# Attention on one core: VectorE's share of the output products put off behind the exchange of maxima, value operands split one place later

## The chip, the core and the metric

The kernel runs on one core of one Trainium2 chip. The core has five engines that work in parallel, each through its own instructions in program order: TensorE (PE; its weight loads are listed as PEld), VectorE (DVE), ScalarE (ACT), GpSimd (POOL) and SyncE (SP), which here does nothing but issue DMA transfers. They wait for one another by semaphores. TensorE reads operands from the on-chip SBUF and writes sums to banks of PSUM. The metric is the time of one execution on the device in microseconds (us); smaller is better.

## The reference

One decoder block over 2048 positions and 1024 channels. The normalized input is multiplied by one wide matrix; from its columns come a recurrent branch and an attention branch, which are projected, merged with sigmoid gates, projected again, added to the input and normalized. What matters here is the attention: eight heads of 128 channels; each position attends to three key sets, windows of 128, 512 and 2048 positions with strides of 1, 4 and 16, and the three results are merged by their softmax denominators:

```
for window, dilation in ((128, 1), (512, 4), (2048, 16)):
    s = q @ kk * HEAD_DIM ** -0.5, masked to the band
    lse = logsumexp(s);  o = exp(s - lse) @ vv
w = softmax(stack(lses));  out = sum(w * stack(outs))
y_attn = (out * silu(z_attn)) @ w_out_attn
merged = sigmoid(g_r + bg_r) * y_rnn + sigmoid(g_a + bg_a) * y_attn
```

Everything is in float32. The kernel holds each operand of a matmul as a pair: a rounded high part and the rest as a low part. One product is then three matmuls (high by high, high by low, low by high).

## The kernel before, in words

A *split* makes such a pair: one engine writes the rounded copy (line 162 on ScalarE, 165 on VectorE), another subtracts it from the original (line 168 on POOL, 171 on VectorE). Because these are helpers, most splits of the kernel carry the same four lines, and the name of the tile tells them apart. `mm3` (lines 156 to 159) issues the three matmuls.

The change lies in the attention stage, about 1375 to 1935 us of the execution. Its order is written out by hand: instructions go to each engine in the order in which the Python program issues them. The main loop (lines 2286 to 2311) runs over steps `s`. There are 16 half heads (`Head` objects: eight heads, each for two halves of the sequence), and each has six units, in the order of `ORDER`: four of kind "c" (one residue of the position modulo 4, which serves the windows of 512 and 2048) and two of kind "w" (the window of 128). In step `s`, TensorE does the scores of unit `s`; VectorE takes their maxima (line 1595) and ScalarE the exponentials (line 1596); seven steps later the probabilities are scaled (line 1660) and transposed (lines 1680 and 1693), and one step after that multiplied with the values (`sums`) into a bank `o`, which VectorE empties by a multiplication with a gate (lines 1719 and 1739).

Work that belongs to a place of a step is listed in a plan by `at(step, place, function)` and issued by `run`. The places in a step, in order:

- HEAD: before the scores of the step;
- SOFTMAX: after the step's maxima and exponentials;
- then most of the step's share of output products (below);
- EXCHANGE: once per half head, that is in every sixth step; one matmul sends the maxima and sums of each key set to the partitions where the other set needs them (`exchange`, line 1752), VectorE reads them (line 1761) and forms the common maxima (`maxima`), ScalarE takes their exponentials (line 1775);
- then the rest of the step's output products;
- WEIGHTS: in the same sixth step, VectorE turns them into the factors `M` (`weights`, lines 1777 to 1784);
- transposes of unit `s - 7` and sums of unit `s - 8`;
- TAIL: among other things the scaling of the unit that is transposed in the next step, and loads.

Keys and queries are split at HEAD and SOFTMAX places (`split_kq`, tiles kraw and kq); at HEAD of two steps POOL regroups the queries of the window of 128 (`window_queries`, line 1557). Values of a unit are loaded (`load_v`, line 1563, one transfer; `load_v1`, line 1581, four) into one of three raw tiles, vraw, in TAIL of the step that is three before their transposes, and split (`split_v` into vh, `split_v1` into wh; ScalarE rounds, POOL subtracts) at TAIL of the step before their transposes. All these loads are issued by SP, one after the other, so a load whose tile is still in use holds up those behind it.

TensorE's spare time in the stage is filled with the *output products* (generator `steps`, from line 1833): y_rnn and y_attn as 128 by 512 tiles, each of eight steps of one `mm3` into a PSUM bank `pj`. `spend` issues as many as are owed: 3.6 per step of the attention, later 3.1. In the course of a tile, at fixed steps, the generator also issues

- the emptying of the tile before: VectorE multiplies its bank with the loaded gate (line 1913) and, for y_attn, adds the other branch's part (line 1915);
- the store of that tile (line 1920) and the load of the next gate (line 1908), both by SP;
- weight loads (line 367), and row loads and splits of the next group's rows (`load_y`, line 1887 or 373; `split_y`, lines 1889 to 1897): ScalarE rounds into yh, and VectorE or POOL, by the row's number, subtracts into yl.

After the attention stage the same generator goes on inside `output_products`.

Of the kernel before, what the change touches and what calls it, by code (L numbers as in the profile page):

```python
# [15 lines left out]
ALU = mybir.AluOpType  # L16
# [73 lines left out]
def decoder_block(ctx, tc, x, c, positions, g_norm, w_mod, b_mod, w_in, b_gate, conv_w, conv_b,  # L90
# [76 lines left out]
    def lo_pool(o, i, h):  # L167
        nc.gpsimd.tensor_tensor(o, i, h.bitcast(F32), ALU.subtract)  # L168

    def lo_dve(o, i, h):  # L170
        nc.vector.tensor_tensor(o, i, h.bitcast(F32), ALU.subtract)  # L171
# [1353 lines left out]
    def at(slot, place, fn, *args):  # L1525
        plan.setdefault((slot, place), []).append((fn, args))

    def run(slot, place):
        for fn, args in plan.pop((slot, place), ()):
            fn(*args)  # L1530

    class Head:
# [273 lines left out]
        def enlist(self, B):  # L1806
            for c, (ld, s, place) in enumerate(((5, 2, HEAD), (5, 2, SOFTMAX), (4, 1, HEAD), (3, 0, HEAD))):
                at(B - ld, TAIL, self.load_kq, c)
                at(B - s, place, self.split_kq, c)
            for i, s in enumerate((B, B + 2)):  # L1810
                at(s, HEAD, self.window_queries, i)
            e = B + NU
            at(e - 1, SOFTMAX, self.gather, 1)
            at(e, HEAD, self.gather, 0)
            at(e, EXCHANGE, self.exchange)
            at(e, EXCHANGE, self.maxima)
            at(e, EXCHANGE, self.exponentials)
            at(e, WEIGHTS, self.weights)
            for u, (kind, x) in enumerate(ORDER):
                s = B + u + LAG  # L1820
                at(s - 1, TAIL, self.scale, kind, x)
                at(s - 1, TAIL, self.split_v if kind == "c" else self.split_v1, x)
                at(s - 3, TAIL, self.load_v if kind == "c" else self.load_v1, x)
            e = B + NU + LAG
            at(B + LAG - 1, TAIL, self.load_gate)
            at(e, TAIL, self.merge, 1)
            at(e + 1, TAIL, self.merge, 3)
            at(e + 2, TAIL, self.store)
# [4 lines left out]
    def steps(jobs):  # L1833
# [55 lines left out]
        def split_y(j, k):  # L1889
            if j < len(jobs):  # L1890
                w, ys, n = jobs[j]
                t = Y0.pop((ys is yaT, n, k), None)
                yh, yl = Y.get((j, k)) or new_y(j, k)
                t = yl[:].bitcast(F32) if t is None else t[:]
                hi_act(yh[:], t)
                on_dve = k not in (3, 4) if j == LAST_HEAD else k % 2 or not j
                (lo_dve if on_dve else lo_pool)(yl[:], t, yh[:])

        def load_g(t):
            j, m = tiles[t]  # L1900
# [9 lines left out]

        def evict(t, ps):
            g = G[t]
            nc.vector.tensor_tensor(g[0][:], ps[:], g[0][:], ALU.mult)
            if len(g) > 1:
                nc.vector.tensor_tensor(g[0][:], g[0][:], g[1][:], ALU.add)

        def store(t):
            j, m = tiles[t]
            w, ys, n = jobs[j]
            nc.sync.dma_start((mrT if ys is yaT else meT)[m * P : (m + 1) * P, n * CH : (n + 1) * CH], G.pop(t)[0][:])  # L1920
# [5 lines left out]
        for t, (j, m) in enumerate(tiles):  # L1926
            ps = T(pj, [P, CH], F32, "pj") if j < LAST_HEAD or t % 4 < 2 else FP["bank"](t % 4 - 2)
            for k in range(KT):
                u = 2 * t + k // KH
                if k % KH == 1:  # L1930
                    if u + 3 < RAW_W - 1:
                        if u + 3 == n_w[0]:
                            load_w(u + 3)
                    elif u == 2 * KT * LAST_HEAD:
                        load_w(RAW_W - 1)
                    if u in raw_at:
                        load_w(raw_at[u])
                    if u in split_at:
                        split_w(split_at[u])
                if k == (1 if j < LAST_HEAD else 3) and t:  # L1940
                    evict(t - 1, last)
                if k == (4 if t == TURN else 3) and t < TURN + 3:
                    load_g(t)
                if k == (7 if j < LAST_HEAD else 6) and t:
                    store(t - 1)
                x = 2 * (KT * min(j, LAST_HEAD) + m) + k // KH
                wt = W[x]
                row = {5: 7, 6: 5, 7: 6}.get(k, k) if t == TURN + 1 else k
                yh, yl = Y[j, row]
                mm3(ps[:], wt[:, 0, row % KH, :], wt[:, 1, row % KH, :], yh[:], yl[:], first=k == 0, last=k == KT - 1)  # L1950
                if k % KH == KH - 1 and (j != LAST_HEAD if m < KT - 1 else j <= LAST_HEAD):
                    W.pop(x)

                step = m * KT + k
                if j < LAST_HEAD:
                    if step in range(KT * KT - 24, KT * KT - 14, 2):
                        load_y(j + 1, (step - KT * KT + 24) // 2)
                    if step == KT * KT - KT - 1:
                        split_y(j + 1, 0)
                    if m == KT - 1:  # L1960
                        if k < 4:
                            split_y(j + 1, k + 1)
                        if j + 1 < LAST_HEAD:
                            if 4 <= k < KT - 1:
                                load_y(j + 1, k + 1)
                        else:
                            if k == 1:
                                load_y(j + 1, 5)
                            if k == 3:
                                load_y(j + 1, 6)  # L1970
                                load_w(n_w[0])
                                load_y(j + 1, KT - 1)
                            if k == KT - 1:
                                split_y(j + 1, KT - 1)
                    if j and m == 0 and k in (0, 2, 3):
                        split_y(j, 5 + (k + 1) // 2)
                else:
                    i = (t - KT * LAST_HEAD) * KT + k
                    if i < 2:
                        split_y(j, 5 + i)  # L1980
                    if i in (0, 1, 2, 3, 5, 6, 7, 8):
                        load_y(LAST_HEAD + 1, i - (i > 3))
                    if i in (4, 5, 6, 7, 10, 11, 12, 13):
                        split_y(LAST_HEAD + 1, i - (4 if i < 8 else 6))
                    if k == KT - 1 and TURN + 2 <= t < len(tiles) - 1:
                        load_g(t + 1)
                yield
            last = ps
# [2 lines left out]

    LAST_HEAD, RAW_W = NB + 2, 2 * KT * (NB + 2) + 4
    n_steps = [0]

    def spend(fill, owed, left):

        while owed >= left + 1:
            next(fill)
            n_steps[0] += 1
            owed -= 1  # L2000
        return owed
# [274 lines left out]
    with tc.manual_schedule():  # L2276
        units = []
        for g in range(2 * H):
            hd = Head(g // H, g % H)
            hd.enlist(NU * g)  # L2280
            units += [(hd, u) for u in ORDER]
        last_head = [hd]
        owed = 0.0
        first = min(s for s, _ in plan)
        end = max(s for s, _ in plan) + 1
        for s in range(first, max(end, len(units) + LAG + 1)):
            rate = FILL[0] if s < NU * H + LAG else FILL[1]
            owed += rate + (MORE if 0 <= s <= NU else 0.0)

            run(s, HEAD)  # L2290
            softmax = None
            if 0 <= s < len(units):
                hd, u = units[s]
                softmax = hd.scores(*u)
            if softmax:
                softmax()
            run(s, SOFTMAX)
            owed = spend(fill, owed, rate / 4)
            run(s, EXCHANGE)
            owed = spend(fill, owed, 0.0)  # L2300
            run(s, WEIGHTS)
            if 0 <= s - LAG < len(units):
                hd, u = units[s - LAG]
                hd.transposes(*u)
            owed = spend(fill, owed, 0.0)
            if 0 <= s - LAG - 1 < len(units):
                hd, u = units[s - LAG - 1]
                evict = hd.sums(*u)
                if evict:
                    at(s + 1, SOFTMAX, evict)  # L2310
            run(s, TAIL)
        owed = spend(fill, (NB + 2) * KT * KT - n_steps[0], 0)
        pools.close("ap", "sc", "pT", "po")
        output_products(fill)
# [29 lines left out]
```

## Time and profile before

| | us |
|---|---|
| three runs | 2197.92, 2202.35, 2202.59 |
| their median | 2202.35 |
| the profiled execution | 2203.34 |
| its span, first to last instruction | 2200.7 |
| TensorE busy | 2161.4 (98%) |
| VectorE, ScalarE, POOL busy | 1488.3, 1261.9, 1237.5 |

The profile is one execution. A page gives the busy time of each engine over the span and the groups of instructions by line; further views answer for a stretch of time: who waited for whom, the instructions of an engine in order of time with the idle time before each and what ended it, and busy time with TensorE's granted clock (1.00 is full speed) by window. A busy TensorE is not TensorE at its peak, because overlapping matmuls are counted to their ends.

### The profile page before, as it was taken

The page shows a single profiled execution, that of the slowest core. Times are in us where ns is not written, and L with a number is a line of the kernel's source. Part 1 is how long each engine was busy: PE and PEld are TensorE (multiplying, and loading weights), DVE is VectorE, ACT ScalarE, POOL GpSimd, SP SyncE. Part 2 cuts the span into 40 slices and gives each one's busy share as a digit, 9 for nine tenths or more (in the row PEclk, how much of TensorE's full clock was granted, in tenths as well). Part 3 has the DMA queues.
Part 4 walks back from the last instruction along what each step waited for, and adds up shares of the span by engine and source line. Part 5 has one row for each costly group of instructions (what it writes and reads, how often), then busy time and mean ns, then how long its engine had stood idle before and what let it go on. Part 6 is the DMA issues. An engine that isn't in the chain of part 4 may idle for free. (4 is left out here: it accounts for less than half of the span.)

```text
span 2200.7 us, 34270 instructions
## 1 busy us (share of the span) xinstructions
PE 2161.4 (98%) x11330; PEld 1838.1 (84%) x11330; DVE 1488.3 (68%) x2453; ACT 1261.9 (57%) x2543; POOL 1237.5 (56%) x910
## 2 busy tenths in 40 slices
PE   8999999999999999999999999999999999999998
PEld 5998888888888998888888887888889898978786
DVE  6678888978576765455545465467677878755876
ACT  4647667667543447557557412567778887632433
POOL 2468767677566355445445223446575656433886
PEclk9999999999999999999999999999999999999999
DMA  8355665665897567787887898989988888799453
GB/s 291 103 172 185 219 198 194 203 209 195 265 274 221 166 191 255 248 250 233 263 258 248 263 286 274 284 267 273 289 272 270 242 257 255 226 291 296 160 164 134
DMA packets 454522, 513.89 MB, mean 234 GB/s; under 512 B 91241, under 2 KB 333637, under 8 KB 453577
## 3 DMA queue, kind: packets, MB, share of 16 engines
q1 hardware_dynamic: 427444, 431.81, 65.2%
q10 hardware_dynamic: 26708, 79.86, 9.4%
q8 instruction: 89, 1.46, 0.3%
q14 instruction: 89, 0.72, 0.1%
q0 software_dynamic: 192, 0.05, 0.0%
HBM read 337.52 MB, written 174.07 MB: 232 GB/s over the span
## 5 line engine op out<-in xcount | busy, mean ns | idle before, releaser
L168 POOL TENSOR_TENSOR S<-R,S 128x512 fp32r<-128x512 f32 x278 | 411.4, 1485 | 372.2 <-ACT S L162 271.2
L154 PE MATMUL V<-T,S 128*128 128x512 f32 x1344 | 324.4, 390 | 0.5 <-DVE xr L482 0.5
L154 PE MATMUL X<-T,S 128*128 128x512 f32 x1344 | 323.3, 389 | 0.3 <-POOL S L168 0.3
L154 PEld LDWEIGHTS X<-T,S 128*128 128x128 f32 x1344 | 252.0, 188 | 52.9 <-POOL S L168 0.7
L154 PEld LDWEIGHTS V<-T,S 128*128 128x128 f32 x1344 | 251.4, 188 | 52.9 <-DVE xr L482 1.0
L154 PE MATMUL pj<-yh,S 128*128 128x512 f32 x848 | 287.6, 397 | 4.4 <-ACT yh L162 3.8
L168 POOL TENSOR_TENSOR S<-s,S 128x512 fp32r<-128x512 f32 x114 | 183.0, 1605 | 103.2 <-ACT S L162 78.7
L162 ACT ACTIVATE S<-R 128x512 fp32r<-128x512 f32 x278 | 171.2, 622 | 117.1 <-DMA R<-in_w_in_dram 77.4
L154 PEld LDWEIGHTS pj<-yh,S 128*128 128x128 f32 x848 | 160.7, 190 | 37.5 <-ACT yh L162 4.7
L1596 ACT ACTIVATE pp<-pp,st 128x256 f32<-128x256 f32 (+3 forms) x256 | 133.4, 523 | 75.4 <-DVE st L1595 75.0
L154 PE MATMUL pj<-yl,S 128*128 128x512 f32 x424 | 167.5, 395 | 2.4 <-DVE yl L171 1.5
L154 PE MATMUL Y<-T,S 128*128 128x512 f32 x672 | 161.5, 389 | 0.0
L154 PE MATMUL W<-T,S 128*128 128x512 f32 x672 | 161.5, 389 | 0.0
L154 PE MATMUL Z<-T,S 128*128 128x512 f32 x672 | 161.4, 389 | 0.0
L154 PEld LDWEIGHTS Z<-T,S 128*128 128x128 f32 x672 | 126.1, 188 | 26.2
L154 PEld LDWEIGHTS Y<-T,S 128*128 128x128 f32 x672 | 126.1, 188 | 26.2
L154 PEld LDWEIGHTS W<-T,S 128*128 128x128 f32 x672 | 126.1, 188 | 26.2
L162 ACT ACTIVATE S<-s 128x512 fp32r<-128x512 f32 x114 | 71.1, 624 | 117.2 <-DVE s L299 61.6
L998 DVE SCALAR_TENSOR_TENSOR xc<-xr,par,xc 128x512 f32<-128x512 f32 x96 | 97.9, 1020 | 50.6 <-ACT xc L992 48.3
L171 DVE TENSOR_TENSOR ptl<-pT,pth 128x384 fp32r<-128x384 f32 (+1 forms) x160 | 97.8, 627 | 49.3 <-ACT pth L162 47.1
L1595 DVE CUSTOM_DVE_ANT_0 pp<-sc,msk 128x256 f32<-128x256 f32 (+3 forms) x256 | 104.2, 449 | 34.7 <-PE sc L154 32.1
L168 POOL TENSOR_TENSOR kq<-kraw,kq 128x512 fp32r<-128x512 f32 (+1 forms) x64 | 101.3, 1594 | 39.8 <-ACT kq L162 30.2
(393 smaller groups left out, 4828.7 us busy)
## 6 DMA issues: line engine op xcount, KB each, us to landing
sD<-S ACTq DMA_DIRECT2D x112, 512.0 KB, 3.6
S<-sD SPq DMA_DIRECT2D x112, 512.0 KB, 4.8
S<-wD SPq DMA_DIRECT2D x100, 512.0 KB, 5.9
R<-in_w_in_dram SPq DMA_DIRECT2D x195, 256.0 KB, 4.2
wD<-s ACTq DMA_DIRECT2D x64, 256.0 KB, 4.5
T<-in_w_mod_dram SPq DMA_DIRECT2D x8, 1024.0 KB, 9.5
vN<-ev SPq DMA_DIRECT2D x64, 128.0 KB, 2.6
zaT<-ev SPq DMA_DIRECT2D x32, 256.0 KB, 3.4
```

Source lines behind the costliest of these rows:

```text
L154: nc.tensor.matmul(o, lhsT=l, rhs=r, start=st, stop=sp, **kw)
L162: nc.scalar.activation(o, i, AF.Copy)
L168: nc.gpsimd.tensor_tensor(o, i, h.bitcast(F32), ALU.subtract)
L171: nc.vector.tensor_tensor(o, i, h.bitcast(F32), ALU.subtract)
L998: nc.vector.scalar_tensor_tensor(xc, xr[:, i : i + CH], cw(i), xc, ALU.mult, ALU.add)
L1595: nc.vector.tensor_tensor_reduce(pdst, s_ps, mask, 1.0, 3e38, ALU.add, ALU.min, m_)
L1596: nc.scalar.activation(pdst, pdst, AF.Exp, bias=m_, scale=-1.0, accum_out=l_)
```

## The change

It has two parts.

First, between the place SOFTMAX and the end of WEIGHTS of a step that has an exchange, VectorE's instructions of the output products are not issued where the generator reaches them, but kept in a list: the low part of a split row (line 171 as called from `split_y`) and the emptying of a finished tile (lines 1913 and 1915). They are issued right after WEIGHTS, in their order, or earlier if a product is about to read such a row or a store is about to send such a tile. Rounding on ScalarE, subtractions on POOL, loads and stores stay where they were. In all other steps nothing is put off.

Second, the values of a unit are split at the place SOFTMAX of the step of their transposes, and not at TAIL of the step before. Their loads stay where they were.

```
             for u, (kind, x) in enumerate(ORDER):
                 s = B + u + LAG
                 at(s - 1, TAIL, self.scale, kind, x)
-                at(s - 1, TAIL, self.split_v if kind == "c" else self.split_v1, x)
+                at(s, SOFTMAX, self.split_v if kind == "c" else self.split_v1, x)
                 at(s - 3, TAIL, self.load_v if kind == "c" else self.load_v1, x)
...
                 on_dve = k not in (3, 4) if j == LAST_HEAD else k % 2 or not j
-                (lo_dve if on_dve else lo_pool)(yl[:], t, yh[:])
+                if on_dve:
+                    on_vector((j, k), lambda: lo_dve(yl[:], t, yh[:]))
+                else:
+                    lo_pool(yl[:], t, yh[:])
...
         def evict(t, ps):
             g = G[t]
-            nc.vector.tensor_tensor(g[0][:], ps[:], g[0][:], ALU.mult)
-            if len(g) > 1:
-                nc.vector.tensor_tensor(g[0][:], g[0][:], g[1][:], ALU.add)
+
+            def gated():
+                nc.vector.tensor_tensor(g[0][:], ps[:], g[0][:], ALU.mult)
+                if len(g) > 1:
+                    nc.vector.tensor_tensor(g[0][:], g[0][:], g[1][:], ALU.add)
+            on_vector(t, gated)

         def store(t):
+            settle(t)
...
                 row = {5: 7, 6: 5, 7: 6}.get(k, k) if t == TURN + 1 else k
+                settle((j, row))
                 yh, yl = Y[j, row]
...
+    put_off, waiting = [False], []
+
+    def on_vector(key, fn):
+        if put_off[0]:
+            waiting.append((key, fn))
+        else:
+            fn()
+
+    def settle(key=None):
+        while waiting and (key is None or any(key == k for k, _ in waiting)):
+            waiting.pop(0)[1]()
...
             run(s, SOFTMAX)
+            put_off[0] = (s, EXCHANGE) in plan
             owed = spend(fill, owed, rate / 4)
             run(s, EXCHANGE)
             owed = spend(fill, owed, 0.0)
             run(s, WEIGHTS)
+            put_off[0] = False
+            settle()
```

## The prediction

> **What bounds the kernel now.** I read four views, in this order: the page, the list of waits of TensorE inside the attention stage, a table of short windows, and the timelines of the engines around each place where TensorE stood. The page first:
>
> ```profile
> span 2200.7 us, 34270 instructions
> PE 2161.4 (98%) x11330; PEld 1838.1 (84%) x11330; DVE 1488.3 (68%) x2453; ACT 1261.9 (57%) x2543; POOL 1237.5 (56%) x910
> ```
>
> TensorE sets the time, so the change can only win what TensorE loses in the stage that it touches, the attention stage from 1375 to 1935 us. Its waits there (engine, line, what released it: us in total, times, longest):
>
> ```profile
> PE pT L1680 <- ACT pp L1660: 2.3, 2, 2.0
> PE sc L154 <- POOL q L1557: 1.5, 3, 0.7
> PE sc L154 <- DVE sm L1748: 1.4, 1, 1.4
> PE sc L154 <- DVE xq L1761: 1.4, 1, 1.4
> PE pj L154 <- POOL yl L168: 0.9, 1, 0.9
> PE pT L1680 <- DVE ptl L171: 0.7, 1, 0.7
> PE o L154 <- DVE zt L1719: 0.4, 1, 0.4
> ```
>
> That is all there is to win directly: 8.6 us in ten stops. The windows show what two of them cost besides (window, its length, then busy us of PE, PEld, DVE, ACT and POOL, granted clock, DMA share, GB/s):
>
> ```profile
> 1438.00:1442.00 4.00, 4.00 (x14) 3.38 (x15) 3.35 (x19) 2.69 (x10) 0.90 (x2) 0.57 0.96 344
> 1834.00:1838.00 4.00, 4.00 (x21) 3.96 (x20) 1.83 (x6) 4.00 (x13) 2.20 (x2) 0.57 0.25 74
> ```
>
> After the stops at 1437 and 1832 the granted clock of the next 4 us is 0.57: each costs another 0.43 x 4 = 1.72 us.
>
> On this the Trainium skill, page "TensorE: Matmul & The Clock Gate", section "The HAM clock gate (the "warmup" mystery)", says that the clock is halved after at least one idle window of about 3.4 us. The trace differs: stops of 1.4 and 2.3 us were enough. By the page's rule these two terms of 1.72 would be absent and the sum below 3.44 us smaller.
>
> **The two stops behind an exchange.** Rows of TensorE, VectorE and ScalarE in order of time (start, length, engine, line, instruction, in brackets the idle time before it and what ended it). First the exchange step at 1434, then the one at 1824:
>
> ```profile
> 1433.93 0.68 DVE L1739 TENSOR_TENSOR yw<-o,zt 128x512 f32<-128x512 f32 x1
> 1435.82 1.70 DVE L171 TENSOR_TENSOR yl<-yl,yh 128x512 fp32r<-128x512 f32 x1 [1.21 <-ACT yh L162]
> 1437.44 0.34 DVE L1761 TENSOR_TENSOR xq<-sc,cs 128x64 f32<-128x64 f32 x2
> 1437.93 1.25 PE L154 MATMUL sc<-kq,q 128*128 128x256 f32 x6 [1.41 <-DVE xq L1761]
> 1439.70 0.17 DVE L1784 SCALAR_TENSOR_TENSOR M<-M,dm 128x16 f32<-128x16 f32 x1
> ```
>
> ```profile
> 1824.11 0.38 PE L154 MATMUL sc<-sm,msk 128*128 128x128 f32 x2
> 1825.67 1.19 DVE L171 TENSOR_TENSOR yl<-R,yh 128x512 fp32r<-128x512 f32 x1 [1.45 <-ACT yh L162]
> 1826.78 0.34 DVE L1761 TENSOR_TENSOR xq<-sc,cs 128x64 f32<-128x64 f32 x2
> 1828.84 0.68 DVE L1913 TENSOR_TENSOR fg<-pj,fg 128x512 f32<-128x512 f32 x1
> 1829.55 0.69 DVE L1915 TENSOR_TENSOR fg<-fg,fg 128x512 f32<-128x512 f32 x1
> 1832.04 0.18 DVE L1784 SCALAR_TENSOR_TENSOR M<-M,dm 128x16 f32<-128x16 f32 x1
> 1832.25 1.23 ACT L1660 ACTIVATE pp<-pp,M 128x384 f32<-128x384 f32 x2 [1.68 <-DVE M L1784]
> 1832.96 0.30 PE L1680 MATMUL pT<-cs,pp 128*128 128x128 f32 x1 [2.04 <-ACT pp L1660]
> ```
>
> Both show one thing: VectorE works in program order, and an output product's subtraction (line 171, tile yl) stands in front of the maxima. VectorE idles until ScalarE has rounded that row, then subtracts, and only then reads the exchanged maxima (line 1761), though they had been in PSUM since 1824.5 in the second case. There a product's eviction (lines 1913 and 1915) also stands in front of the weights (line 1784).
>
> **Part 1: putting off.** Nothing is added or removed: instructions of lines 171, 1913 and 1915 that fall between the softmax and the weights of an exchange step go behind the weights. I ran the loop's own arithmetic (3.6, later 3.1 product steps per attention step): 7 of the 16 exchange steps have such work (steps 12, 18, 30, 36, 42, 66 and 84); in the other 9 nothing changes. The stops above belong to steps 12 and 84.
>
> Step 12: from the first exchanged maximum to the last weight takes 1437.44 to 1439.87, so 2.43 us undisturbed. Without the subtraction in front it can start when VectorE's earlier work (line 1739) ends at 1434.6, 2.8 us sooner. The scores bank is then free before TensorE wants it, near 1436.5. Gain: 1.41 + 1.72 = 3.13 us. What it costs: the subtraction, 1.2 to 1.7 us, now ends near 1438.5, and the product that reads that row comes just there; I put this at nothing, with 0.5 as its worst end.
>
> Step 84: maxima from about 1824.6, weights by 1827.1, the scaling (1.23 us) done by 1829; TensorE wants the transposes at 1830.9. There is 1.9 us of cover, so even a chain stretched by POOL stays hidden. Gain: 2.04 + 0.27 (a second stop of the same kind, the 2.3 of the list) + 1.72 = 4.03 us. Behind the weights now stand 1.2 + 0.68 + 0.69 us of put-off work, then the rest of the step: no later than before, since the whole chain moved up by 5 us. The store of that product waits for its eviction, but comes six product steps after it, over a step of attention.
>
> In the other five steps the chain gets shorter where nothing waited for it: nothing.
>
> **Part 2: the values split later.** Per unit (96 of them) two instructions move: ScalarE's rounding and POOL's subtraction. They carry no DMA. They move past, on ScalarE, the rounding of keys and the step's exponentials; on POOL, the subtractions of keys and the regrouping of window queries (line 1557). What that frees, by POOL's rows before the stop at 1721 (TensorE 0.70, and 0.33 at 1619):
>
> ```profile
> 1717.59 1.30 POOL L168 TENSOR_TENSOR vh<-vraw,vh 128x512 fp32r<-128x512 f32 x1 [1.78 <-ACT vh L162]
> 1718.85 1.84 POOL L168 TENSOR_TENSOR kq<-kraw,kq 128x768 fp32r<-128x768 f32 x1
> 1720.63 1.63 POOL L1557 CAST q<-kq 128x512 fp32r<-128x512 f32 x2
> 1721.76 2.02 PE L154 MATMUL sc<-kq,q 128*128 128x256 f32 x12 [0.70 <-POOL q L1557]
> ```
>
> With the 1.30 us of values behind instead of ahead, the queries end about 1 us sooner, for ScalarE's rounding of the keys comes 0.5 us sooner too. Gain: 0.55 of the 0.70, and the 0.33: 0.9 us.
>
> What it costs. The values' split now follows the exponentials. ScalarE often stands before these:
>
> ```profile
> ACT pp L1596 <- DVE st L1595: 75.0, 43, 3.3
> ```
>
> In 43 of 96 steps the rounding (0.41 to 0.73 us) used to fill that wait and now comes after it, ahead of the rows of the products. No stop hangs on it directly but the last of the list; I take 0.4 us, ends 0 and 2.
>
> SP is the dearer part. The next value load reuses the raw tile that the split frees, and SP issues in order:
>
> ```profile
> SPq L1581 <- POOL vh L168: 68.1, 21, 6.5
> SPq L1563 <- POOL wh L168: 19.6, 20, 3.0
> SPq L1563 <- POOL vh L168: 18.6, 11, 4.0
> ```
>
> So at 52 loads SP already waits for exactly this subtraction, 106 us in all. Later splits make it wait longer. Queued behind are key, gate, weight and row loads. Weights are loaded almost three half tiles ahead, and for a key load ScalarE stood three times only, all in the first heads. The thin ones are the rows of the next product group, three loads at each change of group:
>
> ```profile
> ACT kq L162 <- DMA kraw<-qT: 4.9, 3, 3.3
> 1602.35 0.43 SPq L1563 DMA_DIRECT2D vraw<-vN  x1
> 1834.07 1.28 POOL L168 TENSOR_TENSOR vh<-vraw,vh 128x512 fp32r<-128x512 f32 x1 [2.69 <-ACT vh L162]
> 1839.62 1.34 SPq L1887 DMA_DIRECT2D yl<-oT x2
> DMA to landing us min/median/max: 3.2/6.1/7.2
> 1846.23 1.14 ACT L162 ACTIVATE yh<-yl 128x512 fp32r<-128x512 f32 x2
> 1430.56 0.63 ACT L162 ACTIVATE yh<-yl 128x512 fp32r<-128x512 f32 x1 [2.65 <-DMA yl<-yaT]
> 1433.51 0.49 PE L154 MATMUL sc<-sm,msk 128*128 128x128 f32 x2 [1.43 <-DVE sm L1748]
> ```
>
> The last two rows price a late row: ScalarE stood 2.65 us for it and TensorE then 1.43, so the first 1.22 us are covered. In the change of group near 1605 the value load of 1602.35 moves to about 1603.9 (exponentials, then the split), the rows behind it with it: 1.5 us late, 0.3 of it not covered. At 1839 the load stands behind the split at 1834.07. That one will follow the exponentials, which I place at 1832.9 after the change, and end near 1834.8: hardly sooner than now, though TensorE arrives 4 us sooner. The rows then land near 1839.6 + 6.1 = 1845.7, and ScalarE, which took them at 1846.23, will want them near 1842.2. Late by 3.5 us (ends 0 and 4.5), so 2.3 after the cover. At 1430 SP does not hang on the values; that stop stays, as do the 0.9 and the 0.7 of the list.
>
> **Sum.** -3.13 - 4.03 - 0.9 + 0.4 + 0.3 + 2.3 = -5.1 us. The profiled execution took 2203.34 us, 2200.7 its span; the median of the runs is 2202.35, 1.0 below. So 2198.2 for a like execution, 2197.3 for the median. With no late rows and the small stops gone too (0.9 + 0.7 + 0.4) it is 2192.3.
>
> The Trainium skill, page "GPSIMD Engine Reference", section "Specifications", has POOL share SBUF interfaces with VectorE instructions of two SBUF inputs. The rows agree as far as they go: the subtraction of two SBUF tiles above takes 1.70 and 1.19 us, the eviction from PSUM 0.68. It speaks against part 2, which sets 1.3 us of POOL beside the weights; the 1.9 us of cover would bear that.
>
> **Rivals.**
> *The late rows take back the gain.* If three changes of group (1430, 1605, 1839) each come 2.5 us late, each costs 1.3 and a slow clock of 1.72: 9.0. That gives 2202.35 - 8.06 + 0.4 + 9.0 = 2203.7. For it: the 106 us on SP. Against it: at 1430 SP hangs on other things.
> *Slower: SP becomes the bound at the changes of group.* If the value loads hold SP 4 us, those three cost 2.8 + 1.72 each, and a fourth, near 1515, half as much: 15.8, and 2210.5. It decides, by more than 4.4 us, from a delay of about 3 us. For it: single waits of 6.5 and 4.0 us already. Against it: at 1602 I worked out 1.5.
> *Nothing changes.* One run of three took 2197.92: stops like these may come and go, and the median need not hold them. Then 2202.
> *The clock is no part of it.* If the two slow stretches came with or without the stops, only the stops are won: 4.6, with 3.0 lost, so 2200.7. That each slow window directly follows a stop speaks against it. It is also what the clock page of the Trainium skill would give.
>
> **Numbers.** Forecast 0.57, late rows 0.13, slower 0.16, nothing 0.09, no clock 0.05. I take 0.2%, 4.4 us, as what a measurement tells from no change: faster 0.57, same 0.27, slower 0.16. The range, 2192.3 to 2204, runs from all small stops gone to the first rival and leaves out the slow one and a little more.
>
> **What would show it.** Right: no wait of TensorE for line 1761 nor for line 1660, no window at 0.57 near 1438 and 1834; line 1761 directly behind the exchange's matmul; waits for line 1557 under 0.3 us. SP's waits for the values' subtraction above 106 us. Wrong: new waits of ScalarE for row loads longer than 3 us, or TensorE waiting for a value split (tiles vh, wh), which now has some 3 us of cover.

## The result, and the profile after

| | us |
|---|---|
| before, median of 21 runs beside the change (2196.36 to 2203.69) | 2200.73 |
| after, median of 21 runs (2197.25 to 2210.71) | 2203.92 |
| ratio, 95% interval | 1.0016 [1.001, 1.0023] |
| profiled execution after, span | 2210.71, 2208.9 |

The change made the kernel slower by 0.16%. That is less than the 0.2% that the prediction took as measurable; with this many runs the interval excludes no change all the same. The forecast was 5 us faster.

From the head of the page after: all engines have the work of before, to within some 4 us.

```profile
PE 2164.8 (98%) x11329; PEld 1839.7 (83%) x11330; DVE 1492.6 (68%) x2453; ACT 1263.4 (57%) x2543; POOL 1236.3 (56%) x910
```

TensorE's waits in the attention stage after the change (engine, line, what released it: us in total, times, longest):

```profile
PE sc L154 <- DVE sm L1748: 5.1, 2, 3.2
PE pT L1680 <- DVE ptl L171: 4.1, 5, 2.0
PE pj L154 <- POOL yl L168: 3.1, 2, 1.9
PE o L154 <- DVE zt L1719: 0.7, 1, 0.7
PE sc L154 <- POOL q L1557: 0.6, 1, 0.6
PE pj L154 <- DVE yl L171: 0.4, 1, 0.4
PE pT L1693 <- DVE ptl L171: 0.4, 1, 0.4
```

The two lines that the change was aimed at are gone, the wait for the exchanged maxima (line 1761) and the one for the scaling (line 1660), and the window queries (line 1557) fell from 1.5 to 0.6. In their place stand 14.4 us in thirteen stops, where 8.6 in ten stood.

This execution was the longest of the 21, and the profiled one of before (2203.34) is near the upper end of its 21 too. So both kernels were profiled a second time, unedited, as experiments of their own; their rows come here because the reading needs them.

> The kernel before once more, for a second profile. If the stops behind the exchanges of steps 12 and 84 belong to the order of the instructions, TensorE stands there again, 1.4 and 2.0 us, and the stage from the first scores to the last sums takes 553 to 556 us. If they hang on how transfers and engines happen to fall in one execution, one of them is missing or under 0.7 us, the half clock behind it too, and the stage takes under 551 us.

It took 2194.14 us, less than any of the 21 runs of before above. The lines of the two exchanges in the same view:

```profile
PE pT L1680 <- ACT pp L1660: 2.1, 2, 1.9
PE sc L154 <- DVE xq L1761: 1.1, 1, 1.1
```

> The whole change once more, for a second profile. By the theory that the order decides: stops again at steps 12 (3.2 us, maxima's sum behind a late row), 30 (1.9), 67 (1.9, POOL's row behind the values) and 85 (2.0, transposes behind put-off work), and a stage of 558 to 562 us. By the theory that single executions differ: one or two of these four are missing, the stage takes 553 to 558 us and the time is near the median of 2203.9.

It took 2200.47 us. The four longest lines of the same view:

```profile
PE pT L1680 <- DVE ptl L171: 4.1, 5, 2.0
PE pj L154 <- POOL yl L168: 2.8, 2, 1.9
PE pj L154 <- DVE yl L171: 1.5, 3, 1.0
PE sc L154 <- DVE sm L1748: 1.4, 1, 1.4
```

The second profile of before has the stops of its first expectation, and the short stage and the missing half clock of its second. The second profile of after fits its second expectation, but for the time: the stop at step 30 is missing, the one at step 12 is 1.4 us and not 3.2, and the stage takes 555.2 us; the stops at steps 67 and 85 are back.

So the stops behind the exchanges do belong to the order of instructions before (1.4 and 2.0 us, then 1.1 and 1.9), and after the change two new ones do, a row of POOL at step 67 and ptl behind the exchange of step 84 (in the transposes of step 85, as the expectation counts it). In the second profile they are

```profile
1730.20 0.50 PE L154 MATMUL pj<-yl,S 128*128 128x512 f32 x1 [1.93 <-POOL yl L168]
1832.54 0.63 PE L1680 MATMUL pT<-cs,pp 128*128 128x128 f32 x4 [2.02 <-DVE ptl L171]
```

and in the first 1.93 and 2.02 as well (rows below). What comes and goes is the wait for line 1748 (5.1 us, then 1.4) and the clock. The table takes the stage from the first scores to the last sums (554.5 us in the first profile). Idle is its length less TensorE's busy time; clock is half the length of its stretches at half clock.

| execution | stage | idle | clock | the rest |
|---|---|---|---|---|
| before, first profile | 554.5 | 9.0 | 3.4 | 542.0 |
| before, second | 550.8 | 7.7 | 0 | 543.1 |
| after, first | 561.9 | 14.5 | 5.1 | 542.3 |
| after, second | 555.2 | 12.2 | 0 | 543.0 |

The rest is constant within 1.1 us, so idle time and clock account for the stage. By these four executions the change adds 3.2 to 6.9 us of idle time, by which two are compared; the medians of the runs differ by 3.2 us.

**Behind the exchange of step 84, where ptl took the place of the scaling.** VectorE, then POOL, after the change, in order of time (start, length, engine, line, instruction; lines 1918 and 1920 are 1913 and 1915 of before):

```profile
1831.84 0.36 DVE L1761 TENSOR_TENSOR xq<-sc,cs 128x64 f32<-128x64 f32 x2 [0.30 <-PE sc L154]
...
1832.87 1.23 DVE L1771 TENSOR_TENSOR dm<-M,st 128x16 f32<-128x16 f32 x1
1834.02 1.32 DVE L1772 TENSOR_TENSOR dm<-M,xs 128x16 f32<-128x16 f32 x1
...
1836.43 1.09 DVE L1784 SCALAR_TENSOR_TENSOR M<-M,dm 128x16 f32<-128x16 f32 x1
1837.44 0.68 DVE L171 TENSOR_TENSOR yl<-R,yh 128x512 fp32r<-128x512 f32 x1
1838.05 0.68 DVE L1918 TENSOR_TENSOR fg<-pj,fg 128x512 f32<-128x512 f32 x1
1838.76 0.69 DVE L1920 TENSOR_TENSOR fg<-fg,fg 128x512 f32<-128x512 f32 x1
1839.37 1.15 DVE L171 TENSOR_TENSOR ptl<-pT,pth 128x512 fp32r<-128x512 f32 x2
```

```profile
1832.78 1.29 POOL L168 TENSOR_TENSOR vh<-vraw,vh 128x512 fp32r<-128x512 f32 x1
1834.03 1.28 POOL L168 TENSOR_TENSOR yl<-yl,yh 128x512 fp32r<-128x512 f32 x1
1836.20 1.29 POOL L168 TENSOR_TENSOR yl<-R,yh 128x512 fp32r<-128x512 f32 x1 [0.90 <-ACT yh L162]
```

```profile
1840.20 0.96 PE L1680 MATMUL pT<-cs,pp 128*128 128x128 f32 x7 [2.02 <-DVE ptl L171]
```

The low part ptl of before, for comparison:

```profile
1832.13 1.15 DVE L171 TENSOR_TENSOR ptl<-pT,pth 128x512 fp32r<-128x512 f32 x2
```

Line 1761 now starts at once, where it started 2.29 us after the exchange's matmul. But the chain to line 1784 takes 1837.52 - 1831.84 = 5.68 us and not the 2.43 of step 12 before: three instructions of 0.17 to 0.18 us take 1.09 to 1.32, and each of them ends with an instruction of POOL (1834.10 with 1834.07, 1835.34 with 1835.31, 1837.52 with 1837.49). The put-off work follows, and only then ptl, which TensorE wants next. From the exchange's matmul to ptl it was 1832.13 - 1824.49 = 7.64 us before; now it is 1839.37 - 1831.81 = 7.56. The same work stands between them in another order. VectorE no longer idles there for the row's rounding (1.2 us) and does the row in 0.7 us and not 1.2, but the chain without the evictions grew from 4.1 to 5.7 us beside POOL, and that took both back.

**Step 67, where values stand in front of a row.** First POOL before the change: the values are done long before the row's rounding.

```profile
1726.06 1.29 POOL L168 TENSOR_TENSOR vh<-vraw,vh 128x512 fp32r<-128x512 f32 x1 [3.79 <-ACT vh L162]
1728.55 1.30 POOL L168 TENSOR_TENSOR yl<-yl,yh 128x512 fp32r<-128x512 f32 x1 [1.20 <-ACT yh L162]
```

ScalarE, POOL and TensorE after the change:

```profile
1732.54 0.61 ACT L162 ACTIVATE vh<-vraw 128x512 fp32r<-128x512 f32 x1
1733.06 1.14 ACT L162 ACTIVATE yh<-yl 128x512 fp32r<-128x512 f32 x2
```

```profile
1733.23 1.29 POOL L168 TENSOR_TENSOR vh<-vraw,vh 128x512 fp32r<-128x512 f32 x1 [6.20 <-ACT vh L162]
1734.48 1.72 POOL L168 TENSOR_TENSOR yl<-yl,yh 128x512 fp32r<-128x512 f32 x1
```

```profile
1736.25 0.50 PE L154 MATMUL pj<-yl,S 128*128 128x512 f32 x1 [1.93 <-POOL yl L168]
```

The values' rounding now follows the exponentials of the step, and POOL, idle for 6.20 us, takes the values first and the row, which a product waits for, second.

**Late rows and SP.** First ScalarE at the steps of 1435 and 1528, then TensorE, then SP's waits for the values' subtraction:

```profile
1431.94 0.63 ACT L162 ACTIVATE yh<-yl 128x512 fp32r<-128x512 f32 x1 [3.39 <-DMA yl<-yaT]
1524.19 0.63 ACT L162 ACTIVATE yh<-yl 128x512 fp32r<-128x512 f32 x1 [2.23 <-DMA yl<-yaT]
```

```profile
1435.63 0.49 PE L154 MATMUL sc<-sm,msk 128*128 128x128 f32 x2 [3.23 <-DVE sm L1748]
1528.24 0.49 PE L154 MATMUL sc<-sm,msk 128*128 128x128 f32 x2 [1.86 <-DVE sm L1748]
```

```profile
SPq L1581 <- POOL vh L168: 90.5, 27, 6.6
SPq L1563 <- POOL vh L168: 35.6, 17, 3.6
SPq L1563 <- POOL wh L168: 20.7, 12, 3.6
```

SP's waits rose from 106 to 147 us. Rows land late at the changes of group near 1430 and 1515; in the second profile of after ScalarE waits for them 2.11 and 0.82 us, and 2.85 near 1611. The wait near 1430 is not the change's alone. In the profiles of kernels that split the values where they were it is 2.65 us (before), 0.7 to 1.1 (before again, part 1 alone, POOL's rows as well) and 3.1 to 3.8 (put off behind the transposes, rows only, tiles only); the two with work added on POOL have 0.3 and 3.8. Only kernels with the whole of part 2 show more than 2 us near 1611, and waits for rows of oT near 1850 (0.6 to 1.2 us).

### The profile page after: what moved, and what is told of

It is laid out like the page before. It is cut to its first block, busy times and chain, and to the rows that moved or that the text cites. A ratio compares the mean times of both kernels' runs of the same rounds, so it can differ in the third digit from the quotient of the medians.

```text
span 2208.9 us, 34265 instructions
## 1 busy us (share of the span) xinstructions
PE 2164.8 (98%) x11329; PEld 1839.7 (83%) x11330; DVE 1492.6 (68%) x2453; ACT 1263.4 (57%) x2543; POOL 1236.3 (56%) x910
## 4 chain that ended last, share of the span: by engine, by line
PE 62%; DMA 7%; DVE 5%; POOL 2%; issue 2%; SPq 1%; ACT 1%; DVEq 0%; ACTq 0%; POOLq 0%
PE X L154 12%; PE V L154 11%; PE pj L154 10%; PE Z L154 6%; PE W L154 6%; PE Y L154 6%; PE sc L154 4%; PE o L154 4%; PE pg L154 1%; PE pT L1680 1%; DMA S<-wD 1%; PE pT L1693 1%; POOL S L168 1%; DMA R<-meT 1%; DMA or<-in_w_o_dram 1%
## 5 line engine op out<-in xcount | busy, mean ns | idle before, releaser
L168 POOL TENSOR_TENSOR vh<-vraw,vh 128x256 fp32r<-128x256 f32 (+1 forms) x64 | 67.0, 1047 | 154.8 <-ACT vh L162 117.1
```

## The experiments

The times, each against runs of the kernel before on the same chip (2198.6 to 2199.3 us in the median), and the stage of the profiled execution, in us as above:

| kernel | ratio, 95% interval | stage | idle | clock |
|---|---|---|---|---|
| part 1 alone | 0.9992 [0.9983, 1.0] | 549.5 | 6.1 | 0 |
| part 2 alone | 1.0014 [1.0003, 1.0024] | 558.9 | 11.6 | 5.1 |
| whole, value loads later too | 1.0001 [0.9992, 1.0011] | 554.2 | 10.3 | 1.7 |
| part 1, put off behind the transposes | 0.9995 [0.9985, 1.0006] | 554.1 | 8.2 | 1.7 |
| part 1, POOL's rows as well | 0.9991 [0.9981, 1.0001] | 549.2 | 5.6 | 1.7 |
| part 1, rows only | 0.9986 [0.9976, 0.9996] | 550.0 | 6.9 | 0 |
| part 1, tiles only | 1.0009 [1.0, 1.0019] | 553.8 | 8.1 | 3.4 |
| part 1, and of part 2 POOL's half | 0.9993 [0.9984, 1.0002] | 550.5 | 7.9 | 0 |

### The two parts, each alone

Part 1 alone is the whole change without this line of its diff, part 2 alone is this line:

```
-                at(s - 1, TAIL, self.split_v if kind == "c" else self.split_v1, x)
+                at(s, SOFTMAX, self.split_v if kind == "c" else self.split_v1, x)
```

> Part 1 alone: VectorE's work is put off behind the weights, the values are split at their old place. If the later split is what cost (values in front of rows on SP, ScalarE and POOL, and beside the weights), this wins most of what was forecast for the two stops: ratio to the kernel before 0.9975 (0.996 to 0.999), no stop for line 1761 or 1660. If the put-off work itself costs, because it stands in front of the low parts of the probabilities, it is slower: 1.001 to 1.003, with stops for tile ptl behind exchanges.

> Part 2 alone: the values are split later, nothing is put off. If the later split is what cost: slower than before by more than the whole change, ratio 1.003 to 1.006, with the stops for lines 1761 and 1660 back and new stops at the changes of row group. If the put-off work is what cost: 0.998 to 1.000, since the queries come sooner.

2196.93 us (0.9992) and 2202.51 us (1.0014). Neither pair of expectations came out whole: part 1 wins less than the first one said and has the stop for ptl of the second, and part 2 alone loses no more than the whole change. Part 1 gains some 2 us and part 2 loses some 3; their sum, 1.0006, is below the whole's 1.0016, but the intervals do not tell them apart. With part 1 alone the longest wait is this:

```profile
PE pT L1680 <- DVE ptl L171: 2.6, 2, 1.9
```

The stop for ptl is there without part 2 (chain of 5.54 us, POOL's instructions beside it adding up to 5.00), so it belongs to the putting off. Part 2 alone shows POOL's row at step 67 (1.48 us) and ScalarE waiting 7.8 us for rows of yaT, with part 1 alone 1.5. The other profiles without part 2 have 0.7 to 5.4 us there, so of this difference only a part is part 2's.

### Value loads later as well

The whole change, and the loads issued where the raw tile has just been freed:

```
-                at(s - 3, TAIL, self.load_v if kind == "c" else self.load_v1, x)
+                at(s - 2, SOFTMAX, self.load_v if kind == "c" else self.load_v1, x)
```

> The whole change, with the value loads issued later as well (at SOFTMAX of the step two before the transposes, where the raw tile is nearly free), so that SP waits less for the split. If late rows through SP cost the gain: 0.998 to 1.000, and SP's waits for vh and wh fall from 147 us to under 70. If the values cost by standing in front of rows on ScalarE and POOL and beside the weights: still 1.001 to 1.002, whatever SP waits.

2199.77 us, 1.0001 [0.9992, 1.0011]. ScalarE's wait for rows of yaT falls from 7.9 to 1.5 us, although SP's waits for values do not fall (154 us): what counts seems to be which loads stand behind them. The wait for line 1748 falls to 0.8 us; the stops at step 67 (1.94 us) and behind the exchange of step 84 (2.02) stay. The time is close to that of the first expectation, but SP's waits are not under 70 us.

By the ratios the later loads win about 3 us (1.0016 less 1.0001). The intervals of the two overlap a little, and the ratios come from different sets of runs. That it is the late rows which cost these 3 us is what the profile suggests, not what the runs show.

### Put off behind the transposes

Part 1 alone, with the list emptied one place further on:

```
             run(s, WEIGHTS)
             put_off[0] = False
-            settle()
             if 0 <= s - LAG < len(units):
...
+            settle()
```

> Part 1 alone, with the put-off work issued behind the transposes and their splits and not in front of them. If the put-off work's place in front of tile ptl costs, it is faster than part 1 alone by 0.1 to 0.2%; if not, within 0.05% of it.

2198.27 us, 0.9995: not better than part 1 alone. The stop of 1.88 us for ptl is gone, but after it the put-off work stands in front of the next unit's maxima: 0.98 us behind line 1595, and 0.27 for the scaling. A late row at 1432 (2.40 us) fell into the same profile, so this run says little on the sum.

### POOL's rows put off too

```
-                if on_dve:
-                    on_vector((j, k), lambda: lo_dve(yl[:], t, yh[:]))
-                else:
-                    lo_pool(yl[:], t, yh[:])
+                on_vector((j, k), lambda: (lo_dve if on_dve else lo_pool)(yl[:], t, yh[:]))
```

> Part 1 alone, with POOL's subtractions of product rows put off behind the weights as well. In the run with part 1 alone the chain from exchanged maxima to weights took 5.54 us in step 84 with POOL at work beside it for 5.00 us, and 2.45 us in step 96 with POOL idle; two of POOL's four instructions there are product rows of 1.29 us. If POOL beside VectorE stretches the chain, it falls to 3.3 to 4.0 us in step 84, the transposes' stop of 1.88 us behind it falls below 1, and the time is 0.998 to 0.9995 of before. If the length comes from something else (the position in the stage, the scores of four small units), it stays at 5.0 to 5.6 us and the time at 0.9992, or 1.000 if POOL's rows now come late themselves.

2196.55 us, 0.9991, and the chain of step 84 stayed at 5.53 us with POOL's instructions beside it adding up to 5.03. This does not speak against POOL: the edit could not move its work. POOL has no other instruction between these places of step 84, so a later place in the program leaves its order as it was, and it starts when ScalarE's rounding is done. The experiment failed as one.

### Rows only, tiles only

Of part 1 only the subtractions of rows, or only the emptying of tiles, goes through the list:

```
-            on_vector(t, gated)
+            gated()
```

```
-                    on_vector((j, k), lambda: lo_dve(yl[:], t, yh[:]))
+                    lo_dve(yl[:], t, yh[:])
```

> Of part 1 only the subtractions of rows on VectorE are put off; finished tiles are emptied where they were. If the gain of part 1 lies in the rows (the subtraction that waits for ScalarE ahead of the exchanged maxima, steps 12 and 84), the time is as with the whole of part 1: 0.9988 to 0.9996 of before, and no wait of TensorE for line 1761. If the emptying of tiles ahead of the weights matters as much, it is 0.9997 to 1.0003, with the scaling in step 84 still waited for by 1 us or more.

> Of part 1 only the emptying of finished tiles is put off; the subtractions of rows stay ahead of the exchanged maxima. With the rows put off alone the time was 0.9986 of before. If the rows carry the gain, TensorE waits for line 1761 near step 12 again (1.1 to 1.4 us) and the time is 0.9996 to 1.0006. If each half of the part is worth something of its own, it is 0.9988 to 0.9995.

2196.58 us (0.9986) and 2200.92 us (1.0009 [1.0, 1.0019]). The rows carry the gain of part 1; putting off the tiles gains nothing. With rows only, no stop is for line 1761, as the first expectation has it, and the stop in step 84 falls from 2.04 to 1.10 us, still for the scaling, as the second has it:

```profile
PE pT L1680 <- ACT pp L1660: 1.1, 1, 1.1
PE pj L154 <- DVE yl L171: 1.1, 2, 0.8
```

The second line is the cost that the prediction put at nothing, a product waiting for a put-off row. With tiles only, the stop in step 84 is for ptl, 2.06 us long. So it is the putting off of tiles that makes ptl what TensorE waits for, and beside the rows it lengthens the stop, from 1.10 to 1.88 us:

```profile
PE pT L1680 <- DVE ptl L171: 2.8, 2, 2.1
```

No wait for line 1761 came back with the tiles only, and that part of the expectation fell: TensorE stood 1.84 us at 1434 for a late row and ran the next 3.4 us at half clock, so it probably reached the maxima too late to wait for them. A profile further down (POOL beside the maxima) has such a stop for a late row too, 2.22 us, but no half clock behind it, and there the wait for the maxima is 1.40 us. Rows only has the lowest ratio of this study; its interval lies wholly below 1 and below that of the change, but overlaps that of the whole of part 1.

### Only POOL's half of part 2

Part 1; ScalarE rounds the values where it did before, and POOL subtracts one place later:

```
-            lo_pool(v[:, 1, :w], t[:, :w], v[:, 0, :w])
+            self.rest["c", c] = lambda: lo_pool(v[:, 1, :w], t[:, :w], v[:, 0, :w])
...
+                at(s, SOFTMAX, lambda kind, x: self.rest.pop((kind, x))(), kind, x)
```

> Part 1, and of part 2 only POOL's subtraction of the values one place later; ScalarE rounds them where it did before. If the new stop at step 67 (TensorE 1.93 us, POOL's row behind values for which ScalarE was late) and the longer holding of the raw tiles come from ScalarE's rounding behind the exponentials, the stop at step 67 is under 0.5 us, SP's waits for the values' subtraction are 100 to 125 us, and the time is 0.9985 to 0.9998 of before. If POOL's place alone does the harm, the stop stays above 1.2 us, the waits are 140 us or more and the time is 1.0005 to 1.002.

2197.26 us, 0.9993. At step 67 POOL's row is in time:

```profile
1722.32 1.28 POOL L168 TENSOR_TENSOR vh<-vraw,vh 128x512 fp32r<-128x512 f32 x1 [2.68 <-ACT vh L162]
1725.83 1.29 POOL L168 TENSOR_TENSOR yl<-yl,yh 128x512 fp32r<-128x512 f32 x1 [2.24 <-ACT yh L162]
```

The stop there is 0.27 us, SP's waits are 125 us, at the upper end of what was expected. So the harm of part 2 is ScalarE's rounding behind the exponentials (1.0016 against 0.9993), not POOL's place. POOL's place has its own small price all the same: the chain of step 84 takes 6.00 us here, the stop for ptl 2.35, and another row of POOL is late by 1.75 us at 1615.

### POOL beside the maxima

The kernel before, with eight additions of 128x192 on POOL in four exchanges, the first one reading what line 1761 has just written; and the same with four additions of 128x448, whose result is written as bf16 and not as fp32 (one execution each):

```
+            if dose[0] in (1, 3, 7, 16):
+                z = T(ap_, [P, 3, 64], F32, "z")
...
+                for _ in range(7):
+                    nc.gpsimd.tensor_tensor(z[:], mask, mask, ALU.add)
```

> The kernel before, with eight added additions of 128x192 on POOL, whose results nobody reads, the first of them waiting for the exchanged maxima, in the exchanges of steps 6, 18, 42 and 96, where POOL did nothing beside the chain in both profiles of the kernel before and the chain took 2.44 to 2.66 us. If POOL beside them is what makes VectorE's small instructions long, the chain takes 4 to 6 us in these four steps, and 2.4 to 3.3 us in the others as before. If the long chains of steps 12, 66 and 84 after the change had another cause, the four stay at 2.4 to 2.7 us.

The chain took 3.30 or 3.31 us in all four steps and changed nowhere else by more than 0.5 us. The cause is shown, but the dose did less than I expected: 0.86 us of the 3.2 that step 84 had. Hence the second run.

> As the run before with added work on POOL in the exchanges of steps 6, 18, 42 and 96, but four additions of 128x448 in place of eight of 128x192: about as much time on POOL in half as many, longer instructions. With the eight short ones (0.58 us each) the chain took 3.30 to 3.31 us in all four steps, against 2.44 to 2.66. If a small instruction of VectorE has to wait until POOL's running instruction ends, the chain grows with their length, to 4 to 5.5 us. If the time on POOL alone matters, it stays at 3.1 to 3.5 us.

5.04 or 5.05 us in all four, with POOL's instructions about 1 us long. VectorE in step 6, then TensorE's new stop behind the exchange of step 96:

```profile
1405.48 0.77 DVE L1779 TENSOR_TENSOR M<-st,xs 128x16 f32<-128x16 f32 x1
1406.37 0.92 DVE L1781 TENSOR_TENSOR dm<-M,xs 128x16 f32<-128x16 f32 x1
```

```profile
1907.98 0.30 PE L1682 MATMUL pT<-cs,pp 128*128 128x128 f32 x1 [1.58 <-ACT pp L1662]
```

Nothing of VectorE's was moved in this kernel: work on POOL alone makes the chain 2.6 us longer and lets TensorE stand 1.58 us at a place where it did not stand before. That it is the length of POOL's instructions, and not the type of their result, which turns 3.30 into 5.04 is argued from the ends that fall together, not tested.

## Why the prediction was wrong, point by point

- **Step 84, the step that failed.** "Weights by 1827.1 ... There is 1.9 us of cover, so even a chain stretched by POOL stays hidden", and the put-off work "no later than before". The chain took 5.7 us, not 2.4. The rows quoted in the prediction could have said it: from 1826.78 to 1832.22 it had taken 5.44 us, and without the two evictions (0.68 + 0.69) still 4.1. The 2.43 us came from step 12, where POOL did nothing beside the chain. The sum left TensorE's next want out, too: ptl, behind the whole list. A stop of 2.02 for ptl stands for one of 2.04 + 0.27 for the scaling; of the 4.03 us, 0.3 came.
- **Step 12.** Right that line 1761 stops holding TensorE: it waits neither in the whole change nor with part 1 alone. The gain of 1.41 was real (1.1 in the second profile of before). The row behind it, put at nothing with 0.5 as its worst end, costs 0.3 to 1.0 us in the profiles where it shows.
- **The clock.** The two terms of 1.72 were no property of the stops: the second profile of before has stops of 1.12 and 1.85 + 0.27 us and no half clock. The last section gives the reason. The rival "the clock is no part of it" had 0.05; its premise for the clock was closer, though not its reason.
- **ScalarE's order.** "No stop hangs on it directly but the last of the list", 0.4 us with 2 as the upper end. The stop of 1.93 at step 67 hangs on it, through POOL's queue. The prediction followed SP's queue behind the values but not POOL's, where rows of products stand behind them. It is the largest new stop that both profiles share beside the one for ptl. Four smaller stops for ptl that no term had (0.70, 0.45, 0.38 and 0.19 us) are in both as well.
- **The queries.** Forecast 0.9 won; 1.5 fell to 0.6 in one profile, to 0 or near it in the other. Right.
- **Late rows.** Right in kind: SP's waits rose past 106 us. The sign named as wrong, ScalarE waiting over 3 us for rows, showed near 1430, but there it shows in kernels without part 2 too. Near 1605 0.3 was forecast, and the stop there grew from 0.92 to 1.15. Near 1839, where 2.3 were put, TensorE stood 0.39 at 1864. The longest came at 1430, called unaffected, and at 1515, which only the slower rival had. The first rival's 2203.7 is close to the median of 2203.92, but not by its sum: it kept both big stops as won.
- **The base.** One profiled execution supplied all terms. Over 21 runs the kernel before took 2200.73, 2.6 us less than it, and the loss of clock in it was 3.4. That the median after, 2203.92, still lies inside the range is luck of this base: against 2200.73 the change loses 3.2 us, where 5.1 were to be won.

## What to carry to other kernels

Before putting work off behind a chain on one engine, ask what stands behind the chain: if the next want of the bound engine is on that same engine, only the name of the wait changes, unless idle time goes away. When a split by two engines is moved, follow every queue that it enters, and look at what the second engine then does first. Price a stop from at least two executions, and separate what is the same to the hundredth in both from what is not.

## What the runs showed of the hardware

**Small VectorE instructions wait for POOL.** A subtraction of 128x16 from two SBUF tiles takes 0.17 us alone and up to 1.32 us beside POOL, and ends when POOL's instruction ends (within 0.03 us in the three rows of step 84). One that starts just ahead of POOL's keeps its length: 0.18 us at 1406.28 in the last run, with POOL starting at 1406.29. The chain of ten grows from 2.44 to 3.30 us with POOL instructions of 0.58 us beside it, and to 5.04 with instructions of about 1 us. The reciprocal (one input, 0.25 us) and line 1761 (from PSUM, 0.34 to 0.36 us) stayed as they were. The Trainium skill, page "GPSIMD Engine Reference", section "Specifications", names this contention for VectorE instructions with two SBUF inputs. The runs agree and add the size.

**Whether a stop costs the clock depends on a grid.** Windows of 3.41 us (window, length, busy us of PE, PEld, DVE, ACT, POOL, granted clock, DMA share, GB/s), first of the kernel before, then of the second profile of after (its grid continued from the half clock ahead of the stage):

```profile
1434.98:1438.39 3.41, 2.00 (x17) 1.78 (x16) 2.47 (x6) 0.81 (x2) 1.99 (x3) 1.00 1.08 230
1438.39:1441.80 3.41, 3.41 (x12) 2.83 (x11) 2.83 (x17) 2.49 (x9) 0.70 (x2) 0.50 0.98 363
1830.93:1834.34 3.41, 1.11 (x8) 0.95 (x9) 3.31 (x14) 2.09 (x5) 0.72 (x2) 1.00 0.40 105
1834.34:1837.75 3.41, 3.41 (x17) 3.41 (x16) 1.24 (x4) 3.41 (x12) 1.68 (x2) 0.50 0.24 72
```

```profile
1828.47:1831.88 3.41, 2.05 (x9) 1.34 (x8) 3.32 (x6) 2.10 (x5) 1.29 (x1) 1.00 0.97 306
1831.88:1835.29 3.41, 2.75 (x23) 2.78 (x24) 2.35 (x10) 1.99 (x9) 0.00 (x0) 1.00 0.32 113
```

In all 14 profiles every stretch at half clock in and shortly after the stage lasts one window of 3.41 us, and they start a whole number of windows apart. After 2.30 us of idle time inside one window (1.11 busy) the next is at half clock. A stop of 2.02 us that falls across a border leaves 1.36 idle in one and 0.66 in the next, and nothing follows. Over these profiles, from 1370 to 1960 us, each of the 16 windows with 1.73 us or more of idle time was followed by half clock, 7 of 19 with 1.25 to 1.58, and none with less. The grid lies elsewhere in each execution, so one and the same stop costs 1.7 us in one and nothing in the next: the stop of 1.88 us for ptl lay in one window with POOL's rows put off too (1.88 idle, then half clock), and across a border with part 1 alone (1.44 idle in the fuller one, no half clock). The Trainium skill, page "TensorE: Matmul & The Clock Gate", section "The HAM clock gate (the "warmup" mystery)", says that the window is 3413 ns and free-running; the runs agree. It also gives an idle window as the condition; here a window idle by half was enough.
